# Transposes of the inverted blocks earlier in VectorE's order, and more streamed products ahead of the recursion and inside the attention levels of a GLA + RWKV-7 + expert layer

## The chip, the cores and the metric

The kernel runs on one core of one Trainium2 chip. The metric is the device time of one execution in microseconds; the median of several runs counts. TensorE (PE in the profile), VectorE (DVE), ScalarE (ACT), GpSimd (POOL) and SyncE (SP, which issues most of the DMAs) each work through their own queue in the order in which the program lists the instructions, and wait for one another through semaphores.

## What is computed

One layer on 256 tokens of width 2048. The input is multiplied by a wide matrix; one part of the columns feeds gated linear attention in two directions, one part feeds an RWKV-7 recursion in two directions, one part gives gates. Both results go through up-projections, an output projection and a layer norm; then 16 experts each choose 32 tokens (three matrices of 2048 x 1024 per expert), and a second layer norm ends it.

```
cols = x @ w_in                                   # 2048 x 10592
y_gla = gla(q, k, v, log_f) + rev(gla(rev(q), rev(k), rev(v), rev(log_b)))
y_rw  = rwkv7(r, w_f, k, v, -kk, kk*a) + rev(rwkv7(rev ...))
    # per token:  sa = S a_t;  S = S * w_t + sa b_t' + v_t k_t';  y_t = S r_t
merged = sigmoid(gate_gla) * (y_gla @ w_up_gla) + sigmoid(gate_rw) * (y_rw @ w_up_rwkv)
x = layer_norm(ALPHA * x + merged @ w_out)
x = layer_norm(ALPHA * x + expert_choice_ffn(x))  # 16 experts: w1, w3, w2
```

## The kernel before

**Two kinds of work.** The large projections (w_in, both up-projections, w_out) are *streamed products*: a generator, `stream`, walks a list of jobs. For each block of 128 rows of a weight matrix ScalarE rounds the block (`whi`, L238), VectorE subtracts to get the rest (`wlo`, L65 with output `wlo`), and TensorE makes three products from the two halves (L275 to L277 with 256 columns per product, or L284 to L286 with 512). The split of a block is put into the queues six blocks ahead of its products (`AHEAD`). The small, dependent work is the *chain*: four groups of four RWKV heads (`rwkv_group`, g = 0 to 3), then two pairs of GLA heads (`gla_pair`).

**How the order is set.** Nothing is scheduled by the compiler: the program order is written out. The chain is a generator that yields a number at each place where it would have to wait for another engine; `run_chain` hands that number to `pump`, which puts streamed products of about that many microseconds into the queues before the chain goes on. A yield may also step a second chain beside it (`side`: the preparation of the next group; `before`: the end of the last group). A larger yield therefore puts more streamed products between two steps of the chain, and these are then missing from what is left when both chains have ended: after them `need("gate7")` and the up-projections run with nothing in between.

**In a group.** Each group inverts triangular 64 x 64 blocks. VectorE solves the 16 x 16 diagonal blocks by substitution (L854 to L864). The result `xn` goes to DRAM (`sc2`) and comes back as 32 x 32 blocks in `nt`, both by DMAs from ScalarE's queue (L871, L876). In the meantime the loop of L867 yields 11 pieces of streamed products (`PIECES`, `SUBST / PIECES` = 1.31 us each); at i = 1 the store is issued, at i = 5 the load. After the loop two VectorE transposes (L881) fill the other half of `nt`, and TensorE combines the blocks: 64 products of 32 x 32 (L889), 64 more (L896), 32 (L910), 32 (L931), with copies by ScalarE and VectorE in between (L890, L897, L900, L912). The finished inverse is `ud`: VectorE's L922 and L937 and ScalarE's L924 and L939 write it. Then comes a yield (L940) and the recursion over four chunks, which begins with 8 products that read `ud` (L969).

```
        for i in range(PIECES):
            yield SUBST / PIECES + side(SIDE1 / PIECES)
```

**In a GLA pair.** Eight levels (L1155), each with two multiplications by VectorE (`scale`), two subtractions (`sums`), four exponentials by ScalarE (`exps`), four 128 x 128 products (L1169) and, from the second level on, two predicated copies by VectorE (L1175). There are two yields per level, 1.22 at L1163 ahead of the products and 0.87 at L1170 behind them.

**The last half.** When all jobs are done, the tokens are routed and the experts' weights are streamed through rings of buffers of 1 MB each; the first of them are loaded during the w_out products and right after (L135, L138, L139).

Of the kernel before, what the change touches and what calls it, by code (L numbers as in the profile page):

```python
# [54 lines left out]
def build(tc, x, w_in, gla_a_up_f, gla_a_bias_f, gla_a_up_b, gla_a_bias_b, gla_norm_g,  # L55
# [6 lines left out]
    mm, act, dve, pool = nc.tensor.matmul, nc.scalar.activation, nc.vector, nc.gpsimd  # L62
# [14 lines left out]
    def bank(tag):  # L77
        return psum.tile([128, 512], F32, tag=tag, name=tag, bufs=4)
# [7 lines left out]
    def S(shape, tag, bufs=1, dt=F32):  # L86
        return (mid if tag in ("t8", "t8b", "x16") else sp if tag in main_tags else cp).tile(shape, dt, tag=tag, name=tag, bufs=bufs)
# [111 lines left out]
    SPREAD, SIDE1, SIDE2, POST, SUBST, PIECES = 0.30, 12.00, 1.00, 1.35, 14.40, 11  # L199
# [558 lines left out]
    def rwkv_group(g, st, ahead, before):  # L758
# [17 lines left out]
        for d in range(2):  # L776
            for p in range(2):

                pvs = [bank("ax").rearrange("p (c f) -> p c f", c=4) for _ in range(2)]
                for c in range(4):  # L780
                    for h in range(2):
                        sl = slice(64 * h, 64 * h + 64)
# [8 lines left out]
            for b in range(2):  # L791
                sl = slice(32 * b, 32 * b + 32)
# [21 lines left out]
        for d in range(2):  # L814
            ps = bank("ax")
            pv = ps.rearrange("q (i p f) -> q i p f", i=4, p=2)
            for i in range(4):
                c = i if d == 0 else 3 - i
# [6 lines left out]
            for p in range(2):  # L825
                for c in range(4):
                    for h in range(2):
                        sl = slice(64 * h, 64 * h + 64)
# [16 lines left out]
        side = ahead()  # L845
# [18 lines left out]
            yield w + side(w * SPREAD)  # L864
        dve.memset(xn.rearrange("p r c -> p (r c)")[:, 16:768:49], 1.0)
        nt = S([128, 2, 16, 32], "t4", 3)
        for i in range(PIECES):  # L867
            yield SUBST / PIECES + side(SIDE1 / PIECES)
            if i == 1:
                for q in range(2):  # L870
                    nc.scalar.dma_start(sc2.rearrange("(q r c) -> q r c", r=32, c=32)[:, 16 * q:16 * q + 16, :],  # L871
                                        xn[64 * q:64 * q + 64, :, 16 - 16 * q:48 - 16 * q])
            if i == 5:

                for d in range(2):
                    nc.scalar.dma_start(nt[64 * d:64 * d + 64, d],  # L876
                                        sc2[32768 * d:32768 * d + 32768].rearrange("(m p c) -> p m c", p=64, c=32))
        flat = lambda t: t.rearrange("p m c -> p (m c)")
        for d in (1, 0):
            sl = slice(64 * d, 64 * d + 64)  # L880
            dve.transpose(flat(nt[sl, 1 - d]), flat(nt[sl, d]))  # L881
        quads = [(64 * d + 32 * b, slice(64 * d + 32 * b, 64 * d + 32 * b + 32)) for d in range(2) for b in range(2)]

        cu = S([128, 2, 16, 32], "t4", 3)
# [30 lines left out]
        for h in range(2):  # L915
            for b in range(2):
                sl = slice(32 * b, 32 * b + 32)
# [9 lines left out]
        for m in range(16):  # L927
            p, c, h = m // 8, m // 2 % 4, m % 2
# [3 lines left out]
        for d in range(2):  # L932
            t_ = slice(32 - 32 * d, 64 - 32 * d)
            for h in range(2):
# [2 lines left out]
                    dve.tensor_copy(ud[o, d, :, :, t_], pv[o])  # L937
                else:
                    act(ud[o, d, :, :, t_], pv[o], AF.Copy)  # L939
        yield 0.60  # L940

        sts = S([128, 2, 2, 128], "t2", T2B)
        yt = S([128, 4, 2, 64], "t2", T2B)
# [6 lines left out]
        for i in range(4):  # L950
            ch = [i, 3 - i]
            if i:
                pv = small()
                for p in range(2):
                    for d in range(2):
                        for h in range(2):
                            sl = slice(64 * h, 64 * h + 64)
# [7 lines left out]
            for p in range(2):  # L965
                for d in range(2):
                    for h in range(2):
                        sl = slice(64 * h, 64 * h + 64)
# [6 lines left out]
            if i < 3:  # L975
                pv = small()
                for d in range(2):
                    for p in range(2):
                        for h in range(2):
                            sl = slice(64 * h, 64 * h + 64)  # L980
# [10 lines left out]
            for d, p, h in dph:  # L991
                sl = slice(64 * h, 64 * h + 64)
                mm(y[sl, d, p, :], am[:, d, p, ch[d], h, 64:128], av[:, ch[d], p, h, :], start=(d + p == 0), stop=(i == 0),
                   skip_group_check=True)
            if i:
                for d, p, h in dph:
                    sl = slice(64 * h, 64 * h + 64)
# [68 lines left out]
    def gla_pair(hp, ld, ahead, side):  # L1066
# [36 lines left out]
        for h in range(2):  # L1103
            for j in range(2):
                sl = slice(j * 128, j * 128 + 128)
# [9 lines left out]
        def sums(s):  # L1115
            DFt, DBt = [S([128, 2, T], "t2p", 4) for _ in range(2)]
            if s == 128:
                tt(DFt[:, :, 0:128], Fc[:, :, 127:128].broadcast_to([128, 2, 128]), Fc[:, :, 0:128], OP.subtract)
                tt(DBt[:, :, 0:128], lg[1][1][:, :, 127:128].broadcast_to([128, 2, 128]), Bx[:, :, 0:128], OP.subtract)
            else:  # L1120
                n = 512 // (2 * s)
                tt(bl(DFt, s), bl(Fc, s), bl(Fc, s)[:, :, s - 1:s].broadcast_to([128, n, 2 * s]), OP.subtract)
                tt(bl(DBt, s), bl(Bx, s), bl(Bx, s)[:, :, s:s + 1].broadcast_to([128, n, 2 * s]), OP.subtract)
            return DFt, DBt

        def exps(s, DFt, DBt):
            qe, ke = [S([128, 2, T], "t2", T2B) for _ in range(2)]
            if s == 128:
                act(qe[:, :, 128:256], Fc[:, :, 128:256], AF.Exp, scale=IT)
                act(ke[:, :, 128:256], Bx[:, :, 128:256], AF.Exp, scale=IT)  # L1130
                act(qe[:, :, 0:128], DBt[:, :, 0:128], AF.Exp, scale=IT)
                act(ke[:, :, 0:128], DFt[:, :, 0:128], AF.Exp, scale=IT)
            else:
                act(bl(ke, s)[:, :, :s], bl(DFt, s)[:, :, :s], AF.Exp, scale=-IT)
                act(bl(ke, s)[:, :, s:], bl(DBt, s)[:, :, s:], AF.Exp, scale=IT)
                act(bl(qe, s)[:, :, s:], bl(DFt, s)[:, :, s:], AF.Exp, scale=IT)
                act(bl(qe, s)[:, :, :s], bl(DBt, s)[:, :, :s], AF.Exp, scale=-IT)
            return qe, ke

        def scale(qe, ke):  # L1140
            tt(ke, ke, k_, OP.mult)
            tt(qe, qe, q_, OP.mult)
            return qe, ke
# [11 lines left out]
        for li, s in enumerate(levels):  # L1155
            qe, ke = sc.pop(0)
            if li + 1 < len(levels):
                sc.append(scale(*ex.pop(0)))
            if li + 2 < len(levels):
                ex.append(exps(levels[li + 2], *df.pop(0)))  # L1160
            if li + 3 < len(levels):
                df.append(sums(levels[li + 3]))
            yield 1.22  # L1163
            ps = bank("ax")
            pv = ps.rearrange("p (h j f) -> p h j f", h=2, j=2)
            for h in range(2):
                for j in range(2):
                    iq = 1 - j if s == 128 else j
                    mm(pv[:, h, j, :], ke[:, h, j * 128:j * 128 + 128], qe[:, h, iq * 128:iq * 128 + 128], start=True, stop=True)  # L1169
            yield 0.87 + side(1.08)  # L1170
            for j in range(2):
                if s == 128:
                    act(att[:, :, j, (1 - j) * 128:(1 - j) * 128 + 128], pv[:, :, j, :], AF.Copy)
                else:
                    dve.copy_predicated(att[:, :, j, j * 128:j * 128 + 128],  # L1175
                                        gmask[:, li - 1:li, :].broadcast_to([128, 2, 128]), pv[:, :, j, :])
            if li == 4:
                nxt = ahead()
        yield side(1e9)
        pos = []  # L1180
        for h in range(2):
            po = bank("ax")
            for vh in range(2):
                for j in range(2):
                    c = h * 256 + vh * 128
# [69 lines left out]
    def all_chains():  # L1255
# [31 lines left out]
        for g in range(4):  # L1287
            yield from rwkv_group(g, state[g], ahead(g + 1), before)
            before = beside(rwkv_post(g, state[g]))
        yield from rwkv_post(3, state[3])  # L1290
        ld = yield from gla_pair(0, state[4]["ld"], lambda: gla_load(1), beside(load_y(1, "am", 1)))
        yield from gla_pair(1, ld, lambda: None, lambda us: 0.0)
        need("gate7")
        chain_pool.close()
# [60 lines left out]
    for r in range(CAP // 8):  # L1355
        sl = slice(r * 8, r * 8 + 8)
# [96 lines left out]
    for gq in range(4):  # L1453
# [38 lines left out]
        if gq == 3:  # L1492
# [7 lines left out]
            for dc in range(4):  # L1500
                sl = slice(dc * 512, dc * 512 + 512)
# [8 lines left out]
        for f, nf, c0, n in down_pieces(gq):  # L1510
            wt = [take() for _ in range(4)]
            for j in range(nf):
                fb = f + j
                for c in range(c0, c0 + n, 512):
                    m = min(512, n)
# [5 lines left out]
            for c in range(c0, c0 + n, 512):  # L1521
                m = min(512, n)
# [32 lines left out]
    for i in range(8):  # L1555
        t2, sl = i % 2, slice(i // 2 * 512, i // 2 * 512 + 512)
# [38 lines left out]
```

## Time and profile before

| | |
|---|---|
| median of 3 runs | 1849.82 us (1841.05 to 1851.86) |
| profiled execution, its own time | 1846.94 us |
| its span | 1845.2 us, so 1.7 us lie around it |
| TensorE busy | 1610.6 us (87%) |
| VectorE busy | 775.2 us (42%) |
| ScalarE busy | 549.7 us (30%) |
| mean granted clock of TensorE | 0.959 of full speed |
| HBM read | 543.24 MB |

The page describes one execution. Busy times are sums over the instructions of an engine; an idle time is put down to what ended it. A line of the timeline gives the start, the length, the engine and line, the operation with output and inputs, the count of merged instructions and, in brackets, the idle time before them with its releaser. A line "(+2 forms)" mixes shapes. L65 is a helper that records every `tensor_tensor`, so it has to be told apart by its tiles.

### The profile page before, as it was taken

Reading aid. Unit: us, or ns where it says so; the run is one execution under the profiler, and the core shown is the slowest. Engines: PE = TensorE matmul, PEld = TensorE weight load, DVE = VectorE, ACT = ScalarE, POOL = GpSimd, SP = SyncE. Lnnn points to the kernel's source line nnn. Section 1 sums busy time; section 2 is a strip of 40 time slices with the busy share of each in tenths; the row PEclk is TensorE's granted clock in tenths of the full one; section 3 lists DMA queues with packets and bytes.
Section 4 is the critical chain, followed back from the end, with each engine's and each line's share of the span. In section 5 each row is a group of like instructions: output and inputs, shape, how many; then the busy total and the mean of one; then the engine's idle time right before and its main releaser. Section 6 shows DMA issues by size and latency. Waiting matters only on the chain.

```text
span 1845.2 us, 27727 instructions
## 1 busy us (share of the span) xinstructions
PE 1610.6 (87%) x11255; PEld 960.0 (52%) x11255; DVE 775.2 (42%) x1400; ACT 549.7 (30%) x1081; POOL 16.4 (1%) x42
## 2 busy tenths in 40 slices
PE   8998999989999999999785998668996779966696
PEld 7997887778677778888631233112331113411122
DVE  6777676667659866665421303111012110111204
ACT  5566354455456755444310001000010000100001
POOL 0000000000000000000000000000000000000000
PEclk9999899999999999999899899889999899998998
DMA  7856363554556558787999999999999999999996
GB/s 210 247 152 191 87 192 111 154 138 139 153 146 209 177 188 272 283 305 253 367 405 422 421 420 420 421 420 421 421 420 421 421 420 421 421 421 420 410 411 248
DMA packets 203114, 561.84 MB, mean 304 GB/s; under 512 B 49804, under 2 KB 100422, under 8 KB 156522
## 3 DMA queue, kind: packets, MB, share of 16 engines
q1 hardware_dynamic: 185008, 557.70, 80.6%
q10 hardware_dynamic: 17978, 2.37, 0.8%
q8 instruction: 88, 1.44, 0.3%
q14 instruction: 40, 0.33, 0.0%
HBM read 543.24 MB, written 16.78 MB: 304 GB/s over the span
## 4 chain that ended last, share of the span: by engine, by line
DMA 43%; PE 19%; DVE 4%; ACT 1%; issue 1%; SPq 0%; DVEq 0%; ACTq 0%
DMA ring_a<-in_w_dram 19%; DMA ring<-in_w_dram 19%; DMA t8b<-in_w_dram 4%; PE mm L284 4%; PE mm L286 4%; PE mm L285 4%; PE mm L1517 2%; PE mm L1468 2%; DVE wlo L65 1%; PE ax L1387 1%; DVE t L65 1%; DVE t2p L65 0%; PE ax L1186 0%; DVE sig L1481 0%; ACT whi L238 0%
## 5 line engine op out<-in xcount | busy, mean ns | idle before, releaser
L65 DVE TENSOR_TENSOR wlo<-wraw,whi 128x512 fp32r<-128x512 f32 (+2 forms) x480 | 311.8, 666 | 194.7 <-ACT whi L238 192.8
L238 ACT ACTIVATE whi<-wraw 128x512 fp32r<-128x512 f32 (+2 forms) x480 | 282.6, 608 | 147.8 <-PE mm L286 63.8
L275 PE MATMUL mm<-x,whi 128*128 128x256 f32 x688 | 209.5, 305 | 3.3 <-ACT whi L238 3.3
L1468 PE MATMUL mm<-ring_a,x 128*32 128x512 f32 x776 | 154.7, 676 | 57.6 <-DMA ring_a<-in_w_dram 57.6
L277 PE MATMUL mm<-x,wlo 128*128 128x256 f32 x688 | 196.7, 286 | 1.5 <-issue 1.5
L276 PE MATMUL mm<-x,whi 128*128 128x256 f32 x688 | 196.8, 286 | 0.0
L1480 DVE TENSOR_SCALAR sig<-sig 64x512 f32<-64x512 f32 x16 | 6.8, 424 | 434.5 <-ACT sig L1478 434.5
L1517 PE MATMUL mm<-ring_a,hid 128*32 128x512 f32 (+1 forms) x524 | 163.6, 601 | 1.5 <-ACT sig L1478 1.3
L284 PE MATMUL mm<-whi,x 128*128 128x512 f32 x384 | 161.6, 421 | 0.0
L1468 PE MATMUL mm<-ring,x 128*32 128x512 f32 x592 | 117.7, 683 | 47.7 <-DMA ring<-in_w_dram 47.5
L285 PE MATMUL mm<-wlo,x 128*128 128x512 f32 x384 | 152.6, 397 | 0.0
L286 PE MATMUL mm<-whi,x 128*128 128x512 f32 x384 | 152.4, 397 | 0.0
L275 PEld LDWEIGHTS mm<-x,whi 128*128 128x128 f32 x688 | 132.9, 193 | 11.9 <-issue 4.1
L65 DVE TENSOR_TENSOR x<-x,ax 128x512 f32<-128x512 f32 (+1 forms) x34 | 22.2, 655 | 270.7 <-PE ax L1527 270.7
L276 PEld LDWEIGHTS mm<-x,whi 128*128 128x128 f32 x688 | 133.2, 194 | 3.2 <-issue 3.1
L277 PEld LDWEIGHTS mm<-x,wlo 128*128 128x128 f32 x688 | 133.2, 194 | 2.0 <-issue 1.7
L1478 ACT ACTIVATE sig<-mm 64x512 f32<-64x512 f32 x16 | 9.4, 588 | 406.5 <-PE mm L1468 406.5
L1517 PE MATMUL mm<-ring,hid 128*32 128x512 f32 x392 | 124.1, 594 | 1.5 <-DMA ring<-in_w_dram 0.8
L1468 PEld LDWEIGHTS mm<-ring_a,x 128*32 128x32 f32 x776 | 29.4, 116 | 162.6 <-DMA ring_a<-in_w_dram 109.3
L1517 PEld LDWEIGHTS mm<-ring_a,hid 128*32 128x32 f32 x524 | 46.2, 111 | 111.9 <-issue 94.7
L1524 ACT ACTIVATE eo<-mm 128x512 f32<-128x512 f32 (+1 forms) x17 | 9.7, 572 | 295.2 <-PE mm L1517 282.3
L1468 PEld LDWEIGHTS mm<-ring,x 128*32 128x32 f32 x592 | 23.5, 117 | 130.9 <-DMA ring<-in_w_dram 89.6
(348 smaller groups left out, 2142.3 us busy)
## 6 DMA issues: line engine op xcount, KB each, us to landing
ring_a<-in_w_dram SPq DMA_DIRECT2D x180, 1024.0 KB
ring<-in_w_dram SPq DMA_DIRECT2D x139, 1024.0 KB
wraw<-in_w_in_dram SPq DMA_DIRECT2D x112, 512.0 KB
t8b<-in_w_dram SPq DMA_DIRECT2D x39, 1024.0 KB
wraw<-in_w_in_dram SPq DMA_DIRECT2D x96, 256.0 KB
wraw<-in_w_out_dram SPq DMA_DIRECT2D x24, 512.0 KB
ring_a<-in_w_dram SPq DMA_DIRECT2D x22, 512.0 KB
wraw<-in_w_up_rwkv_dram SPq DMA_DIRECT2D x16, 512.0 KB
```

What stands on the lines that cost most here:

```text
L65: dve.tensor_tensor(out_, a, b, op=op)
L238: act(hi, raw, AF.Copy)
L275: mm(o, whi[:, sl], hi(k), start=(st0 and cb % 2 == 0), stop=False, skip_group_check=True)
L276: mm(o, whi[:, sl], lo(k), start=False, stop=False, skip_group_check=True)
L277: mm(o, wlo[:, sl], hi(k), start=False, stop=st1, skip_group_check=True)
L284: mm(o, hi(k)[:, sl], whi, start=st0, stop=False)
L285: mm(o, hi(k)[:, sl], wlo, start=False, stop=False)
L286: mm(o, lo(k)[:, sl], whi, start=False, stop=st1)
L1387: mm(ps[:, j * 128:j * 128 + 128], zn[t2][:, dq * 256 + j:dq * 256 + 256:2], ohf[:, t2, gq * 128:gq * 128 + 128], start=(t2 == 0), stop=(t ...
L1468: mm(ps[32 * q:32 * q + 32, :], xe[:, kb, e4 * 32:e4 * 32 + 32], wt[q // 2][:, k, (q % 2) * 512:(q % 2) * 512 + 512], start=(kb == 0), sto ...
L1517: mm(pss[c // 512][32 * e4:32 * e4 + 32, c % 512:c % 512 + m], hids[e4][:, fb % 4, fb // 4, :], wt[e4][:, j, c - c0:c - c0 + m], start=(fb ...
L1524: act(eo[:, 0:m], pss[c // 512][:, c % 512:c % 512 + m], AF.Copy)
```

## The change

Three edits. (1) The two transposes go into the loop of pieces: for the groups 0 to 2 they are recorded at i = 8, two pieces sooner than before; for group 3 the loop gets two more pieces and the transposes stand at i = 10, behind as many pieces as before. (2) The yield ahead of the recursion goes from 0.60 to 2.00. (3) The second yield of each GLA level goes from 0.87 to 1.60. From the first edit on the line numbers of the changed kernel are higher by one. No operation is added or taken out.

```
         nt = S([128, 2, 16, 32], "t4", 3)
-        for i in range(PIECES):
+        flat = lambda t: t.rearrange("p m c -> p (m c)")
+        for i in range(PIECES + 2 * (g == 3)):
             yield SUBST / PIECES + side(SIDE1 / PIECES)
...
-        flat = lambda t: t.rearrange("p m c -> p (m c)")
-        for d in (1, 0):
-            sl = slice(64 * d, 64 * d + 64)
-            dve.transpose(flat(nt[sl, 1 - d]), flat(nt[sl, d]))
+            if i == 8 + 2 * (g == 3):
+                for d in (1, 0):
+                    sl = slice(64 * d, 64 * d + 64)
+                    dve.transpose(flat(nt[sl, 1 - d]), flat(nt[sl, d]))
...
-        yield 0.60
+        yield 2.00
...
-            yield 0.87 + side(1.08)
+            yield 1.60 + side(1.08)
```

VectorE, group 0, around the transposes: rows with `-` are before, with `+` after. `wlo` is a split of the stream, `shs` and `shd` are the evacuation of a finished job, L731 belongs to the preparation of group 1.

```order
-L731 SCALAR_TENSOR_TENSOR t_2487<-ld,prm,t_2338 128x256 x2
-L65 TENSOR_TENSOR wlo<-wraw,whi 128x512 x2
-L65 TENSOR_TENSOR shs<-ppad 128x256
-L330 SCALAR_TENSOR_TENSOR shd<-shs,der,shd 128x256
-L881 STREAM_TRANSPOSE t_2269<-t_2269 64x512 x2
+L882 STREAM_TRANSPOSE t_2269<-t_2269 64x512 x2
+L731 SCALAR_TENSOR_TENSOR t_2489<-ld,prm,t_2338 128x256 x2
+L65 TENSOR_TENSOR wlo<-wraw,whi 128x512 x2
+L65 TENSOR_TENSOR shs<-ppad 128x256
+L330 SCALAR_TENSOR_TENSOR shd<-shs,der,shd 128x256
```

Six instructions that stood ahead of the transposes now stand behind them; in the groups 1 and 2 they are four (L731 twice and two splits). On TensorE the L889 products of group 0 keep their place.

TensorE, group 1, from the last products of the inversion (L931, L932 after the change) to the first of the recursion (L969, L970), before:

```order
L931 MATMUL ax_4230<-t4_3976,t2_4197 32x32 x32
L284 MATMUL mm_4150<-whi_3938,x16_89 128x512
L285 MATMUL mm_4150<-wlo_3939,x16_89 128x512
L286 MATMUL mm_4150<-whi_3938,x16_90 128x512
L969 MATMUL ax_4272<-t4_3390,ud_404 64x64 x8
```

The same place after:

```order
L932 MATMUL ax_4242<-t4_3992,t2_4212 32x32 x32
L284 MATMUL mm_4078<-whi_3956,x16_89 128x512
L285 MATMUL mm_4078<-wlo_3957,x16_89 128x512
L286 MATMUL mm_4078<-whi_3956,x16_90 128x512
L284 MATMUL mm_4077<-whi_3976,x16_89 128x512
L285 MATMUL mm_4077<-wlo_3977,x16_89 128x512
L286 MATMUL mm_4077<-whi_3976,x16_90 128x512
L284 MATMUL mm_4078<-whi_3976,x16_89 128x512
L285 MATMUL mm_4078<-wlo_3977,x16_89 128x512
L286 MATMUL mm_4078<-whi_3976,x16_90 128x512
L970 MATMUL ax_4294<-t4_3409,ud_404 64x64 x8
```

Three streamed products have become nine. Group 3 has the same counts; in the groups 0 and 2, whose streamed products are half as wide, six become eighteen.

VectorE, one level of the first GLA pair, from one set of predicated copies to the next, before:

```order
L1175 COPY_PREDICATED t_7336<-gmask,ax 128x2x128 x2
L65 TENSOR_TENSOR t_7506<-t_7506,ld 128x512
L65 TENSOR_TENSOR t_7505<-t_7505,ld 128x512
L65 TENSOR_TENSOR t2p<-av 128x512
L65 TENSOR_TENSOR t2p<-t_7334 128x512
L65 TENSOR_TENSOR wlo<-wraw,whi 128x512
L1175 COPY_PREDICATED t_7336<-gmask,ax 128x2x128 x2
```

The same level after:

```order
L1176 COPY_PREDICATED t_7418<-gmask,ax 128x2x128 x2
L65 TENSOR_TENSOR t_7591<-t_7591,ld 128x512
L65 TENSOR_TENSOR t_7590<-t_7590,ld 128x512
L65 TENSOR_TENSOR t2p<-av 128x512
L65 TENSOR_TENSOR t2p<-t_7416 128x512
L65 TENSOR_TENSOR wlo<-wraw,whi 128x512
L334 TENSOR_SCALAR shd<-shd 128x512
L65 TENSOR_TENSOR wlo<-wraw,whi 128x512
L1176 COPY_PREDICATED t_7418<-gmask,ax 128x2x128 x2
```

One more split stands in the level, and here also a step of a job's evacuation (L334) that came later before. On TensorE nine or twelve streamed products stood between the L1169 products of two levels; now there are twelve or fifteen. Behind the last chain TensorE's list held 459 streamed products of 512 columns up to the first transpose of the merged activations (L1237, L1238 after); now it holds 366.

## Rows read from the trace of the kernel before

**Rows 1.** The page, the span in 40 slices.

```profile
PE   8998999989999999999785998668996779966696
PEclk9999899999999999999899899889999899998998
DMA  7856363554556558787999999999999999999996
```

**Rows 2.** Stretches: us; busy PE, PEld, DVE, ACT, POOL; PEclk; DMA share; GB/s.

```profile
140.00:560.00 420.00, 395.10 (x4952) 334.04 (x4951) 285.55 (x558) 220.21 (x437) 2.75 (x10) 0.96 0.52 149
...
655.00:890.00 235.00, 234.10 (x1149) 196.46 (x1149) 142.29 (x242) 118.56 (x215) 0.00 (x0) 1.00 0.79 267
...
910.00:1800.00 890.00, 719.93 (x3389) 212.19 (x3390) 129.05 (x147) 51.05 (x102) 0.00 (x0) 0.95 1.01 419
```

**Rows 3.** Waits of PE from 100 to 900 us: us in total, times, longest.

```profile
PE ax L889 <- DVE t L881: 14.7, 4, 7.5
PE ax L1169 <- DVE t L65: 4.1, 7, 1.1
PE ax L969 <- DVE ud L937: 4.0, 8, 0.9
```

**Rows 4.** Timeline of PE at L889, groups 0 to 3.

```profile
181.63 1.92 PE L889 MATMUL ax<-t,moff 32*32 32x32 f32 x124 [7.51 <-DVE t L881]
...
284.98 1.20 PE L889 MATMUL ax<-t,moff 32*32 32x32 f32 x120 [1.69 <-DVE t L881]
...
388.71 1.02 PE L889 MATMUL ax<-t,moff 32*32 32x32 f32 x59 [4.24 <-DVE t L881]
...
482.19 0.25 PE L889 MATMUL ax<-t,moff 32*32 32x32 f32 x4 [0.76 <-DMA t<-sc]
483.74 1.50 PE L889 MATMUL ax<-t,moff 32*32 32x32 f32 x118 [1.30 <-DVE t L881]
```

**Rows 5.** Timeline of DVE: group 0, group 1 (one row), group 2.

```profile
176.05 0.87 DVE L731 SCALAR_TENSOR_TENSOR t<-ld,prm,t 128x256 f32<-128x256 f32 x2
...
180.87 1.44 DVE L881 STREAM_TRANSPOSE t<-t 64x512 f32<-64x512 f32 x2
...
280.21 0.88 DVE L731 SCALAR_TENSOR_TENSOR t<-ld,prm,t 128x256 f32<-128x256 f32 x2
...
383.95 0.88 DVE L731 SCALAR_TENSOR_TENSOR t<-ld,prm,t 128x256 f32<-128x256 f32 x2
...
387.95 1.44 DVE L881 STREAM_TRANSPOSE t<-t 64x512 f32<-64x512 f32 x2
```

**Rows 6.** DMA packets of ScalarE's queue (q10) from 383.2 to 383.5 us.

```profile
q10 hardware_dynamic: 20, 0.00, 5.3%
```

**Rows 7.** Stretches as in Rows 2, shorter.

```profile
167.00:174.00 7.00, 7.00 (x63) 6.87 (x61) 4.76 (x7) 5.59 (x11) 0.00 (x0) 1.00 0.63 164
181.60:187.30 5.70, 5.67 (x163) 5.38 (x167) 2.82 (x5) 2.66 (x5) 0.00 (x0) 0.50 0.01 4
197.60:204.40 6.80, 6.72 (x61) 5.93 (x61) 1.12 (x2) 2.43 (x6) 0.00 (x0) 0.50 0.07 23
286.30:289.70 3.40, 3.40 (x27) 3.18 (x31) 1.29 (x2) 2.24 (x4) 0.00 (x0) 0.51 0.28 104
402.00:405.00 3.00, 2.03 (x21) 1.58 (x22) 0.93 (x3) 1.22 (x4) 0.00 (x0) 1.00 0.63 175
680.00:710.00 30.00, 30.00 (x131) 24.19 (x130) 15.56 (x24) 18.46 (x31) 0.00 (x0) 1.00 0.71 223
```

**Rows 8.** Timeline of PE from L931 to L969, group 1.

```profile
298.64 0.75 PE L931 MATMUL ax<-t,t 32*32 32x32 f32 x64
...
301.17 0.32 PE L969 MATMUL ax<-t,ud 64*64 64x64 f32 x2 [0.87 <-DVE ud L937]
301.71 1.33 PE L969 MATMUL ax<-t,ud 64*64 64x64 f32 x14 [0.22 <-DVE ud L937]
```

**Rows 9.** The GLA pairs: one stretch as in Rows 2; timeline of DVE and PE in a level.

```profile
560.00:655.00 95.00, 88.92 (x440) 71.23 (x439) 86.03 (x158) 66.23 (x146) 0.00 (x0) 1.00 0.58 178
...
579.19 0.70 DVE L65 TENSOR_TENSOR wlo<-wraw,whi 128x512 fp32r<-128x512 f32 x1
...
578.23 1.13 PE L1169 MATMUL ax<-t,t 128*128 128x128 f32 x8 [1.06 <-DVE t L65]
```

## The prediction

> **What bounds the kernel now.** I read the slices of the page first, then the stretches, then TensorE's waits, and then the timelines at the places of the three edits. The slices show two halves [rows 1]: up to about 890 us TensorE is at eight or nine tenths nearly everywhere, behind that the DMA engines are full. The stretches put numbers to it [rows 2]. From 910 to 1800 us the DMA share is 1.01 at 419 GB/s: the experts' weights set the pace there, and the change touches nothing of that half. From 655 to 890 us, behind the chains, TensorE is busy 234.1 of 235 us while the DMA share is 0.79: there the streamed products set the pace. From 140 to 560 us, in the four groups, TensorE is busy 395.1 of 420 us, so 24.9 us are idle, and its mean granted clock is 0.96. [...]
>
> So the first half ends when TensorE has done a fixed amount of work, and ends sooner by every microsecond of its idle time or half speed that goes. The second half starts from the last streamed products and should move up as a whole. That is my step from a stall to the end: one to one.
>
> The waits [rows 3] name what the idle time belongs to: 14.7 us for the transposes (four waits), 4.0 us for `ud` ahead of the recursion, 4.1 us (seven waits) in the GLA levels.
>
> **The transposes, groups 0 to 2.** In group 0 VectorE came to L731 at 176.05 and to the transposes only at 180.87 [rows 5]; TensorE stood until 181.63 [rows 4]. With the six instructions behind them the transposes start at 176.05. TensorE needs the first alone, half of 1.44 us, so it goes on at 176.8: 4.8 us less. In group 1 the place is reached at 280.21 and both are done at 281.7, ahead of the 283.3 at which TensorE begins its wait of 1.69 us: 1.7 us less. In group 2 the place is reached at 383.95; the new order has one split more ahead of it, 0.70 us [rows 9], so the first is done at 385.4 where TensorE waited until 388.71: 3.3 us less.
>
> **Group 3.** The transposes stay behind as many pieces; two pieces of 1.31 us follow, so TensorE arrives 2.6 us later and the two waits of 0.76 (the block's landing) and 1.30 us are covered: 2.1 us less, with work that the tail then lacks. The first edit gives 4.8 + 1.7 + 3.3 + 2.1 = 11.9 us.
>
> **What comes late next.** In group 0 L731 (0.87 us), two splits (1.4 us) and a part of an evacuation, about 3 us together, now run between the transposes and VectorE's next chain step. In the profile they ran while TensorE stood. `ud` may then be late and some of the gain return as a wait at L969: between 0 and 3 us; VectorE has idle time there (busy 285.6 of 420 us in the stretch [rows 2]), so I take the middle, 1.5 us. In the groups 1 and 2 L731 and the splits are 2.3 us and I take nothing, as the four blocks from L889 to L931 leave VectorE longer than that.
>
> **Ahead of the recursion.** Six streamed products of 512 columns more per group, or twelve of 256. One of 512 takes 30/131 = 0.23 us, one of 256 columns 7.0/63 = 0.11 us [rows 7], so 1.4 us per group. TensorE's L969 waits for copies whose time does not depend on it: in group 1 from L931's end at 299.39 to L969's at 303.04 it has 3.65 us [rows 8], with three products in it. The idle time shown is 0.87 + 0.22 us; more hides in the 14 products that took 1.33 us. The gain per group lies between 1.0 (the 4.0 us over four groups) and 1.4: I take 1.25, 5.0 us in all.
>
> **The GLA levels.** Three products more per level on TensorE, 0.70 us, and half a split on VectorE, 0.35 us [rows 9]. VectorE is busy 86.0 of 95 us there and ends most of TensorE's waits [rows 3, 9], so a level in which TensorE waits becomes 0.35 us longer while TensorE does 0.70 us more: 0.35 us gained. With seven such waits that is 2.5 us, with those of other names up to the 6.1 us that TensorE idles in the whole stretch; if VectorE falls behind elsewhere, nothing. I take 3.0.
>
> **The clock.** In group 0 it was at half speed from 181.6 to 187.3, behind the stall of 7.51 us, and again from 197.6 to 204.4, behind the wait at L969; in group 1 from 286.3, behind the wait of 1.69 us [rows 7]. [...] The wait in group 2 at L969, as long as the others, brought no drop (402 to 405 us, 1.00) [rows 7]. So an idle spell of that kind does not decide alone, and I don't take it all back: 0.5 us in group 0 at L889, where 3 us of stall remain, two thirds of 5.1 us at the other L889 places, a third of 6.8 us at L969, as its small products stay: 0.5 + 3.4 + 2.3 = 6.2 us. Ends: 0 and 14.7.
>
> [...]
>
> **Queues that are moved past.** The added products bring their loads forward on SP's queue, in front of the GLA pairs' inputs; the DMA share of 0.52 in the groups and 0.58 in the GLA stretch [rows 2, 9] leaves room, and I cost it at nothing. If that cover went, a GLA pair would begin one load late.
>
> **The sum.** 11.9 - 1.5 + 5.0 + 3.0 + 6.2 = 24.6 us off the 1846.9 us of the profiled execution gives 1822.3. The median of the runs lies 2.9 us higher; I forecast 1823. With every term at its best end (11.9 + 5.6 + 6.1 + 14.7) it would be 1809.
>
> **Rivals.**
>
> *The waits move along (20%).* VectorE does no less, and its late work turns up at L896, L910 and L969. For it: in the GLA stretch it is the fuller engine. Against: outside it is busy two thirds of the time. Half of the first edit, 4 us of the second, no clock: 10 us less, 1837.
>
> *The end is set elsewhere (8%).* The fillers only leave the tail, and the tail is as long for another reason. For it: the second half is all DMA. Against: in the tail TensorE is busy without a gap, the DMA engines are not. 1847.
>
> *The transposes block VectorE (7%), slower.* Now a transpose can reach the head of the queue before its block has landed, and the splits behind it wait too. In group 2 packets of the load still ran between 383.2 and 383.5 [rows 6], half a microsecond ahead of 383.95. A landing 4 us later makes the place as bad as before; from there on each microsecond costs one, once TensorE has used up the six blocks split ahead. Landings 10 us later in three groups cost 3 x 6 = 18 us, less the 8 us of the other edits: 1857. Against: the load has kept to its time in all four groups. [...]
>
> **Chances and range.** My forecast holds with 65%, its own range 1811 to 1832. A measurement of this kernel tells about 1% from no change: faster by over 1% is below 1831.3. Nearly all of the forecast and a tenth of the first rival lie there: 0.65. Within 1%, where the rest of the first rival and the second lie: 0.28. Slower: 0.07. The range up to the first rival and a little beyond is 1811 to 1842.
>
> **What would show it.** Right: the four L889 waits on the transposes fall to under 1 us each; L969 waits under 0.5 us per group; from 140 to 560 us a mean clock of 0.98; the second half starts some 25 us sooner with the same DMA rate. Wrong: L889's idle time now ends on the DMA (third rival), comes back at L896 or L969 (first), or the DMA-bound half grows by what the first loses (second).

## The result and the profile after

The changed kernel takes 1819.51 us (median of 4 runs, 1815.26 to 1821.73); the kernel before, on the same chip, 1846.2 us (1841.05 to 1851.86). The ratio is 0.9854, with an interval from 0.9831 to 0.9876: 26.7 us less, where 1823 us and a sum of 24.6 us were forecast. The profiled execution took 1819.94 us with a span of 1818.2 us, 27.0 us less than the profiled one of before.

The page, the span in 40 slices, answers to [rows 1]; the eights of TensorE in the fourth and the ninth slice, where the groups 0 and 2 waited for their transposes, are nines now:

```profile
PE   8999999999999999999776997668986679966696
PEclk9999999999999999999899999889999899998998
```

The stretches (columns as in [rows 2]). Everything behind the groups comes sooner, so they are cut earlier:

```profile
140.00:545.00 405.00, 394.58 (x4996) 334.24 (x4995) 290.04 (x567) 225.65 (x449) 2.76 (x10) 0.99 0.56 159
...
635.00:866.00 231.00, 231.00 (x1158) 195.08 (x1158) 147.38 (x258) 118.54 (x221) 0.00 (x0) 1.00 0.79 265
886.00:1780.00 894.00, 725.48 (x3409) 212.75 (x3407) 127.98 (x146) 51.06 (x102) 0.00 (x0) 0.95 1.01 419
```

In the groups TensorE is now idle for 405.00 - 394.58 = 10.4 us instead of 24.9. The tail is still without a gap, and the half that the DMA engines pace runs at the same 419 GB/s. TensorE's waits from 100 to 890 us, against [rows 3]:

```profile
PE ax L1170 <- DVE t L65: 6.6, 2, 4.0
...
PE ax L890 <- DVE t L882: 5.4, 2, 2.9
...
PE ax L897 <- issue: 1.9, 2, 1.6
PE ax L783 <- DVE am L65: 1.9, 1, 1.9
```

The transposes' share fell from 14.7 to 5.4 us, the recursion's 4.0 us (now L970) left the list, and the GLA levels' 4.1 us in seven waits became 6.6 us in two, both ahead of the first level of a pair. The timeline of TensorE at L890, groups 0 to 3, against [rows 4]:

```profile
175.81 1.43 PE L890 MATMUL ax<-t,moff 32*32 32x32 f32 x106 [2.48 <-DVE t L882]
...
275.17 1.29 PE L890 MATMUL ax<-t,moff 32*32 32x32 f32 x128
...
372.03 1.29 PE L890 MATMUL ax<-t,moff 32*32 32x32 f32 x128
...
465.40 0.25 PE L890 MATMUL ax<-t,moff 32*32 32x32 f32 x4
...
468.58 1.25 PE L890 MATMUL ax<-t,moff 32*32 32x32 f32 x124 [2.93 <-DVE t L882]
```

Groups 1 and 2 wait no more, group 0 waits 2.48 us instead of 7.51. In group 3 the wait got longer. VectorE's transposes come there at 467.81, behind splits that wait for ScalarE (VectorE stands 3.60, 0.23 and 1.37 us ahead of them). ScalarE's timeline in that place:

```profile
453.65 1.34 ACTq L872 DMA_DIRECT2D sc<-xn  x2
...
460.48 1.32 ACTq L877 DMA_DIRECT2D t<-sc  x2
461.90 1.16 ACT L238 ACTIVATE whi<-wraw 128x512 fp32r<-128x512 f32 x2 [3.67 <-issue]
```

L877, the issue of the block's load, reads what the store writes: it comes at 460.48, 0.7 us behind the store's last packets (by 459.8). It stands in ScalarE's queue ahead of the roundings: ScalarE stood 3.67 us, 1.32 of them the issue itself (the rounding begins 0.1 us behind its end), and the splits of VectorE, the transposes and TensorE's products followed late. The kernel before has the same order, but there the load is issued 4.7 us behind the store and not 6.8:

```profile
471.96 1.34 ACTq L871 DMA_DIRECT2D sc<-xn  x2
...
476.66 1.32 ACTq L876 DMA_DIRECT2D t<-sc  x2
```

The DMA queues in the stretch in which the store's packets ran (packets, MB, share of the 16 engines), first after the change (456.5 to 460 us), then before it (473.5 to 476 us). q10 is ScalarE's queue with the store, q1 is SP's with the weights:

```profile
q1 hardware_dynamic: 477, 0.91, 67.5%
q10 hardware_dynamic: 2080, 0.26, 48.1%
```

```profile
q10 hardware_dynamic: 2057, 0.26, 69.4%
q1 hardware_dynamic: 82, 0.14, 14.9%
```

Before, the weights had 14.9% beside the store's 69.4%; after the change they had 67.5% beside its 48.1%, and the store took longer: its last packets ran 4.1 us behind its issue before (by 476.1 us) and 6.1 us after.

The first transpose of the merged activations comes 25.2 us sooner (770.13 to 744.92 us), and so do the first products of the routing (902.38 to 877.17). Counted on TensorE up to the routing, the tail behind the last pair's levels is 21.8 us shorter (244.78 to 222.94), the four groups are 16.9 us shorter (418.26 to 401.34), and the two GLA pairs are 14.3 us longer (120.87 to 135.21), since they now hold streamed products that the tail held; 0.8 us lie ahead of the groups. From the routing to the end it is 942.8 us before and 941.0 after.

### The profile page after: what moved, and what is told of

It is laid out like the page before. It is cut to its first block, busy times and chain, and to the rows that moved or that the text cites. A ratio compares the mean times of both kernels' runs of the same rounds, so it can differ in the third digit from the quotient of the medians.

```text
span 1818.2 us, 27708 instructions
## 1 busy us (share of the span) xinstructions
PE 1600.9 (88%) x11255; PEld 955.3 (53%) x11255; DVE 773.4 (43%) x1400; ACT 548.6 (30%) x1081; POOL 16.5 (1%) x42
## 4 chain that ended last, share of the span: by engine, by line
DMA 40%; PE 39%; DVE 5%; ACT 2%; issue 1%; SPq 0%; ACTq 0%; DVEq 0%
DMA ring<-in_w_dram 18%; DMA ring_a<-in_w_dram 17%; PE mm L284 7%; PE mm L285 6%; PE mm L286 6%; PE mm L1518 5%; DMA t8b<-in_w_dram 4%; PE mm L1469 2%; PE mm L275 2%; PE mm L277 1%; PE mm L276 1%; PE ax L1170 1%; DVE wlo L65 1%; DVE t L65 1%; ACT whi L238 1%
## 5 line engine op out<-in xcount | busy, mean ns | idle before, releaser
L275 PE MATMUL mm<-x,whi 128*128 128x256 f32 x688 | 206.9, 301 | 2.9 <-ACT whi L238 2.9
L277 PE MATMUL mm<-x,wlo 128*128 128x256 f32 x688 | 194.4, 283 | 0.8 <-issue 0.8
L276 PE MATMUL mm<-x,whi 128*128 128x256 f32 x688 | 194.7, 283 | 0.0
L275 PEld LDWEIGHTS mm<-x,whi 128*128 128x128 f32 x688 | 131.0, 190 | 12.3 <-issue 5.1
L276 PEld LDWEIGHTS mm<-x,whi 128*128 128x128 f32 x688 | 131.1, 191 | 2.9 <-issue 2.9
L277 PEld LDWEIGHTS mm<-x,wlo 128*128 128x128 f32 x688 | 131.0, 190 | 0.3 <-DVE wlo L65 0.3
```

The costliest lines, as they stand in the source:

```text
L275: mm(o, whi[:, sl], hi(k), start=(st0 and cb % 2 == 0), stop=False, skip_group_check=True)
L276: mm(o, whi[:, sl], lo(k), start=False, stop=False, skip_group_check=True)
L277: mm(o, wlo[:, sl], hi(k), start=False, stop=st1, skip_group_check=True)
```

## The experiments

Each kernel was timed beside the kernel before on its own chip; a ratio is to that.

**The three edits apart.** Each edit alone, and the first two together.

```
e1: only the loop with the transposes at i = 8 (i = 10 in group 3)
e2: only   -  yield 0.60              +  yield 2.00
e3: only   -  yield 0.87 + side(1.08) +  yield 1.60 + side(1.08)
e4: the change without the edit of e3
```

> The first edit alone. My reckoning (each edit stands by itself, TensorE's idle time goes one to one): 11.9 us of waits at L889, less 1.5 that come back at L969, plus about 4 us of clock: some 14 us less than before. Rival (the waits move along): the L969 and L896 waits grow by what L889 loses, 6 us less or none.

Measured: 1830.37 us, ratio 0.9929 (0.9909 to 0.9949), 13 us less than 1843.84.

> The second edit alone. My reckoning: 5 us of waits at L969 and about 2 us of clock, 7 us less than before. Rival (the products only leave the tail, and the chain gets longer by as much): no change.

Measured: 1835.79 us, ratio 0.9951 (0.9933 to 0.9968), 9 us less by the ratio, 8 by the medians. The waits of each, TensorE from 100 to 890 us; first e1, then e2:

```profile
PE ax L970 <- DVE ud L938: 3.5, 5, 1.7
...
PE ax L890 <- DVE t L882: 1.7, 1, 1.7
```

```profile
PE ax L889 <- DVE t L881: 16.2, 4, 6.9
```

Each edit removes its own wait and leaves the other's standing, with one exception, group 3. With the first edit alone TensorE comes to L890 there without a wait:

```profile
467.90 1.43 PE L890 MATMUL ax<-t,moff 32*32 32x32 f32 x128
```

With the second alone its waits there are 0.62 and 4.86 us instead of 0.76 and 1.30, and the load is issued 7.9 us behind the store; TensorE and ScalarE of e2:

```profile
476.78 1.45 PE L889 MATMUL ax<-t,moff 32*32 32x32 f32 x92 [4.86 <-DVE t L881]
```

```profile
460.74 1.34 ACTq L871 DMA_DIRECT2D sc<-xn  x2
468.68 1.32 ACTq L876 DMA_DIRECT2D t<-sc  x2
```

> The third edit alone. My reckoning: 3 us less than before. Rival, from the trace of the changed kernel (the first level of each GLA pair waits 2.6 and 4.0 us there, and the clock falls behind these waits): the levels lose what they gain, between no change and 3 us more than before; the first-level waits stand in this profile too.

Measured: 1845.06 us, ratio 1.0011 (0.9998 to 1.0024): nothing gained. TensorE in e3: its wait at the second pair's first level, and the stretch from that wait on.

```profile
636.21 2.05 PE L1169 MATMUL ax<-t,t 128*128 128x128 f32 x8 [3.75 <-DVE t L65]
```

```profile
635.40:642.20 6.80, 5.99 (x18) 5.15 (x19) 6.80 (x13) 5.58 (x16) 0.00 (x0) 0.50 0.41 114
```

Inside the levels TensorE's waits at L1169 fall from 4.1 to 1.1 us, but ahead of the second pair's first level it waits 3.75 us, where the kernel before waits 1.57, and in the stretch that begins in this wait it is at half speed for 6.8 us (granted clock 0.50, 5.99 us busy), which I estimate to cost half of the busy time, 3.0 us.

> The first and the second edit without the third. My reckoning: 21 us less than before, 3 us slower than the full change. Rival, as in the run with the third edit alone: the third edit is worth nothing or costs up to 3 us, so this one comes out equal to the full change or up to 3 us faster; if the first-level waits of the GLA pairs come from the third edit, they are gone here.

Measured: 1820.92 us, ratio 0.9871 (0.9856 to 0.9887), 22.9 us less by the medians. The first two add up within the intervals (13 + 9 = 22). The whole change has 0.9854 and, run again, 0.9857; the intervals overlap. So the third edit adds between nothing and about 3 us beside the others; in the profiles pairs and tail together are 360.4 us without it and 358.1 and 357.0 with it.

The first-level waits are not gone without the third edit. The first pair's in e1, then in e4:

```profile
549.78 1.49 PE L1170 MATMUL ax<-t,t 128*128 128x128 f32 x8 [2.22 <-DVE t L65]
```

```profile
545.63 2.04 PE L1170 MATMUL ax<-t,t 128*128 128x128 f32 x8 [2.62 <-DVE t L65]
```

Run by run, in us: TensorE's waits ahead of the first products of the inversion in group 3, the time from the store's issue to the load's there, and TensorE's wait ahead of the first level of each pair.

| run | edits in it | group 3 | store to load | pair 1 | pair 2 |
|---|---|---|---|---|---|
| before | none | 2.06 | 4.7 | 0.37 | 1.57 |
| e1 | first | none | 4.5 | 2.22 | 1.43 |
| e2 | second | 5.48 | 7.9 | 2.47 | 3.66 |
| e3 | third | 2.13 | 4.7 | 0.37 | 3.75 |
| e4 | first and second | 1.77 | 6.6 | 2.62 | 1.94 |
| the change | all | 2.93 | 6.8 | 2.61 | 4.01 |
| f1, the change again | all | 2.33 | 7.5 | 2.62 | 4.02 |

The late load of group 3 is in every run with the second edit and in no other (in the runs below it is 6.6 to 8.4 us). The wait ahead of the first pair comes with the first or the second edit, not with the third; the one ahead of the second pair grows with the second alone and with the third.

**The whole change again, and what is left in it.**

```
f1: the change
f2: ahead of the first level   -  yield 1.94               +  yield 5.00
f3: -  if i == 8 + 2 * (g == 3):   +  if i == 8:
f4: -  if i == 8 + 2 * (g == 3):   +  if i == 6 + 4 * (g == 3):
```

> The full change once more, on the chip of the next three kernels. Theory (the edits add up: 13 us for the transposes and 9 us for the recursion measured alone, nothing for the levels): 22 us less than before. Rival (the third edit is worth something only when the stalls ahead of it are gone): 25 to 27 us less.

Measured: 1820.14 us, 0.9857 (0.9834 to 0.9879).

> The full change, and the yield of 1.94 that stands one level ahead of the first products of a GLA pair is 5.00: about five halves more, 3.3 us of streamed products, in front of the first level of each pair. Theory (the first level waits for VectorE, 2.6 and 4.0 us in the changed kernel, because TensorE gets there too soon, and the clock falls behind both waits, 10.2 us at half speed): both waits fall under 1 us and most of the 5 us of clock come back, 8 us less than the full change. Rival (VectorE is the bound of the stage, and each added product brings a split that puts the first level off by as much): the waits stay above 2 us, no change.

Measured: 1816.81 us, 0.9844 (0.9819 to 0.9869), not to be told from f1. TensorE's waits in the pairs of f2:

```profile
PE ax L1170 <- DVE t L65: 2.9, 3, 1.0
PE ax L1187 <- DVE t L1176: 2.2, 1, 2.2
```

The two long waits at the first levels are gone, but 5.1 us stand at later levels and behind the last. Pairs and tail together are 357.1 us, as in f1 (357.0): filling this gap moved it. The waits fell as the theory had it, the time did not.

> The full change with the transposes of group 3 also at i = 8, four pieces ahead of the products that need them. Theory (the 2.9 us wait there comes from splits ahead of the transposes that wait for ScalarE): the wait falls to 1.5 us or less, and the drop of the clock behind it may go too, 1.5 to 3 us less than the full change. Rival (the blocks land too late for that): the wait is the same and ends on the DMA, no change.

Measured: 1818.51 us, 0.9849 (0.9824 to 0.9874). The wait of group 3 at L890 is gone from the list (L890 has one wait left, 2.5 us in group 0), the time is not to be told from f1. Most of the wait comes back a little further on, at L897 and L911 of the same group: 0.95 and 0.98 us, where f1 has 0.17. With the edit of f2 as well (g2):

> The full change with more products ahead of the first level (1.94 becomes 5.00) and with the transposes of group 3 at i = 8, both together. Theory (the GLA stage is bound by VectorE, so the first is worth at most the clock behind the first-level waits, 3 us; the second 2.9 us of wait): 3 to 5 us less than the full change. Rival (the waits move to other levels and to L897): no change.

Measured: 1816.65 us, 0.9846 (0.9826 to 0.9865): the lowest median of all, within the interval of the change itself. Here, too, there are waits at L897 and L911 of group 3 (1.46 and 0.98 us) and at later levels, as the rival has it.

> The full change with the transposes of the groups 0 to 2 at i = 6, one piece behind the issue of the load, so that they reach the head of VectorE's queue some 3 us ahead of the landing. Rival of the prediction (a transpose that waits for its blocks holds the splits and the chain behind it): VectorE idles 3 us per group on the DMA and TensorE loses about as much, 5 to 9 us slower than the full change. Theory (six blocks split ahead cover it): VectorE idles as long, TensorE does not, within 3 us of the full change.

Measured: 1826.25 us, 0.9887 (0.9859 to 0.9916), 6 us above f1; on the same chip each of its four runs (1821.70 to 1827.99) is slower than each of f1's (1816.61 to 1821.40). Group 1 of f4 shows the whole chain; the rows are of VectorE, of ScalarE, and of TensorE:

```profile
275.72 1.44 DVE L882 STREAM_TRANSPOSE t<-t 64x512 f32<-64x512 f32 x2 [3.07 <-DMA t<-sc]
277.10 1.19 DVE L716 TENSOR_TENSOR_SCAN t2p<-rstr,t2p 128x520 f32<-128x520 f32 x1
...
278.32 0.64 ACT L726 ACTIVATE t2p<-t2p 128x520 f32<-128x520 f32 x1 [3.18 <-DVE t2p L716]
...
283.08 0.57 ACT L891 ACTIVATE t<-ax 128x512 f32<-128x512 f32 x1
...
283.71 1.22 PE L897 MATMUL ax<-t,t 32*32 32x32 f32 x121 [1.40 <-ACT t L891]
```

VectorE stands 3.07 us on the load; the scan behind the transposes is late by that; ScalarE's L726 waits 3.18 us for the scan, and L891, which stands behind it in ScalarE's list, begins only at 283.08; TensorE, which has its L890 products done at 280.0, waits 1.40 us at L897. Over three groups VectorE loses 8.6 us to the load and TensorE 8.3 us at L897.

**Is VectorE the bound in the GLA pairs?** Two ways of taking 16 multiplications of 0.68 us off it; h1 leaves them out, so it computes something else:

```
g1: -  tt(ke, ke, k_, OP.mult)   +  pool.tensor_tensor(ke, ke, k_, op=OP.mult)
g3: g1 and f3 together
h1: -  tt(ke, ke, k_, OP.mult)   +  pass
```

> The full change, and one of the two multiplications of each GLA level (ke by k) on GpSimd instead of VectorE: VectorE loses 16 x 0.6 = 10 us of work in a stage in which it is busy without a gap between the first and the last level of a pair. Theory (VectorE is the bound of the GLA stage, so filler there only moves TensorE's idle time of about 6 us from one level to another): TensorE's waits in the levels and at the first levels fall from 6.6 to under 2 us, the drops of the clock behind the first-level waits go, 5 to 10 us less than the full change. Rival (the waits come from the length of a level's own chain of steps, not from VectorE's load; GpSimd takes 1.27 us for such an operation where VectorE takes 0.67): the waits stay or grow, no change or slower.

Measured: 1825.89 us, 0.9899 (0.9881 to 0.9917); the waits at L1170 grew to 11.0 us.

> The multiplication on GpSimd and the transposes of group 3 at i = 8. Theory: 7 to 12 us less than the full change, the fastest of all. Rival: as for the two parts, no change.

Measured: 1821.81 us, 0.9876 (0.9858 to 0.9894). Timelines of g1 in a level, GpSimd and then VectorE:

```profile
554.59 1.83 POOL L1142 TENSOR_TENSOR t<-t,ld 128x512 f32<-128x512 f32 x1 [2.28 <-DMA wraw<-in_w_in_dram]
559.97 1.82 POOL L1142 TENSOR_TENSOR t<-t,ld 128x512 f32<-128x512 f32 x1 [3.55 <-ACT t L1136]
```

```profile
554.59 2.38 DVE L65 TENSOR_TENSOR wlo<-wraw,whi 128x512 fp32r<-128x512 f32 x2
...
561.23 1.10 DVE L65 TENSOR_TENSOR t<-t,ld 128x512 f32<-128x512 f32 x1
```

Where GpSimd works, VectorE's two splits take 2.38 us instead of about 1.3, its multiplication 1.10 instead of 0.68; GpSimd's own takes 1.71 us in the mean over 16, against 1.27 for its two 128x512 instructions at L1565. So g1 gave VectorE's load back as longer instructions, and decides nothing about the bound. Hence h1:

> All three edits, and the multiplication of ke by k in the scaling of the GLA levels (one of the two there, 128x512, 0.68 us each on VectorE, 16 of them) is left out, so VectorE has 10.9 us less to do in the GLA pairs and GpSimd has nothing more. Theory (VectorE's work ends TensorE's waits in the GLA pairs after the third edit): TensorE's waits at L1170, 6.6 us with all three edits, fall under 2 us, the half-speed stretches behind the first levels (10.2 us) go, and the whole is 5 to 10 us shorter than with all three edits, about 1810 to 1815. Rival (the first level waits for the chain's own latency, whatever VectorE's load): the waits at L1170 stay at 5 us or more and the time stays at 1817 to 1821.

Measured: 1819.08 us, 0.9869 (0.9836 to 0.9902), the time of the whole change. TensorE's waits at L1170, two of 5.4 us together, and the eight levels of both pairs (columns as in [rows 2]):

```profile
545.21 1.47 PE L1170 MATMUL ax<-t,t 128*128 128x128 f32 x8 [2.01 <-DVE t L65]
...
617.89 2.05 PE L1170 MATMUL ax<-t,t 128*128 128x128 f32 x8 [3.41 <-DVE t L65]
```

```profile
545.20:574.80 29.60, 29.59 (x150) 25.07 (x151) 26.15 (x49) 20.63 (x46) 0.00 (x0) 0.94 0.75 235
617.90:647.30 29.40, 29.40 (x149) 25.07 (x150) 25.89 (x49) 20.69 (x46) 0.00 (x0) 0.95 0.59 179
```

The rival's numbers came. TensorE is busy 29.59 of 29.60 us in the levels, VectorE 26.15. With the third edit the levels are TensorE's, and taking work from VectorE buys nothing there. The two waits at the first levels stand ahead of them, in the preparation. There h1 takes out one multiplication per pair (the scaling of the first level stands ahead of the loop of levels), 0.68 us, and each wait is 0.60 us shorter (2.61 to 2.01, 4.01 to 3.41); in g1, where GpSimd does it in 1.8 us, they are 1.6 us longer than in f1 (4.18 and 5.65). So these two waits hang on VectorE's own instructions in the preparation, and not on latency alone, as the rival had it.

## Why the prediction was right, and where it was not

**One to one to the end: right.** The tail begins and ends without a gap, the first transpose of the merged activations comes 25.2 us sooner, the end 27.0 us. The 1.8 us between the two lie behind the routing, where nothing was changed: that part took 942.8 us before, 941.0 after, and 941.6 to 944.5 in the other profiles. So 25.2 us are the edits' and 1.8 are scatter. The rival by which the end is set elsewhere is out.

**The transposes: right in size, wrong in group 3.** Waits of 11.9 us and about 3.9 us of the clock, less 1.5, were to go, some 14; alone the edit gives 13. Group 0 keeps 2.48 us (3 was said), groups 1 and 2 none. The sign that I named, all four waits under 1 us, was stricter than my own sum, which left 3 us in group 0. That the two waits of group 3 "are covered" holds for the first edit alone (e1: no wait there), and fails beside the second: the wait went from 2.06 us (0.76 + 1.30) to 2.93. What failed is the term on the queues, "I cost it at nothing". With the second edit the load behind the store of group 3 is issued 6.6 to 8.4 us after the store instead of 4.5 to 4.7, and alone the edit makes the wait 5.48 us; in the profile of the change the weights had 67.5% of the DMA engines beside that store (14.9% before), ScalarE stood 3.67 us at L877, and the splits and the transposes came late on VectorE. That the late load comes from the second edit is shown by the runs; that it is the loads brought forward which slow the store is my reading of the two queues, and no run moves those loads by themselves. f3 removes the wait at L890, of which 1.9 us return at L897 and L911.

**The 1.5 us that I let return at L969: did not come** beside the second edit; no wait of L970 is left. Alone, the first edit leaves 3.5 us there (e1), no more than the 4.0 of before, though group 3's grew from 1.07 to 1.70. The rival by which waits move along is too large for the first two edits, which give 13 and 8 to 9 us by themselves, but its mechanism is there in all three: 2 us more ahead of the first GLA pair with either of the first two, group 3's wait with the second, and the second pair's first level with the third.

**Ahead of the recursion: right.** 5.0 us and 2.3 of the clock were forecast, 8 to 9 measured, with an interval from 6 to 12.

**The GLA levels: right inside them, wrong in front of them.** I wrote that "a level in which TensorE waits becomes 0.35 us longer while TensorE does 0.70 us more", and added that up over the levels to 3.0 us. The levels did close: alone the edit takes 3.0 us off their waits (e3), and in the whole change TensorE has no wait inside them any more. But the sum ended at the last level. Alone, the edit made the wait in front of the second pair's first level 2.2 us longer, the granted clock was 0.50 for 6.8 us from within that wait on, and the time is what it was. Beside the others it is worth nothing to 3 us. In the whole change the waits in front of the two first levels grew from 1.94 to 6.62 us, by 4.7, which I had at nothing; of these the first pair's 2.2 come with the first two edits (e1, e2, e4), not with the third. The timelines of TensorE in the profile of the whole change:

```profile
548.16 1.09 PE L1170 MATMUL ax<-t,t 128*128 128x128 f32 x4 [2.61 <-DVE t L65]
...
621.47 2.05 PE L1170 MATMUL ax<-t,t 128*128 128x128 f32 x8 [4.01 <-DVE t L65]
```

VectorE's instructions in the preparation set the length of these waits (h1 and g1), and its work inside the levels ahead does not: ahead of the second pair's wait h1 takes out the eight multiplications of the first pair and one in the preparation, and the wait falls by about one, 0.60 us. Why TensorE and VectorE come to this place some 2 us further apart in one run than in another is not settled; e2 waits 3.66 us ahead of the second pair and e4, which has the first edit as well, 1.94.

**The clock: right in size, by two errors.** 6.2 us were to come back. The stretches at half speed (a granted clock of 0.50) in the profile after, columns as in [rows 2]:

```profile
176.20:179.60 3.40, 3.40 (x110) 3.34 (x99) 3.04 (x7) 3.40 (x8) 0.00 (x0) 0.50 0.35 81
227.40:230.80 3.40, 3.40 (x47) 3.06 (x43) 2.25 (x5) 0.00 (x0) 0.00 (x0) 0.50 0.26 39
469.80:473.20 3.40, 3.40 (x10) 2.72 (x9) 1.66 (x4) 2.88 (x5) 0.00 (x0) 0.50 0.59 204
548.30:551.70 3.40, 3.40 (x13) 3.01 (x14) 3.40 (x7) 1.56 (x7) 0.00 (x0) 0.50 1.08 369
620.00:626.80 6.80, 5.33 (x17) 4.59 (x18) 6.80 (x13) 5.13 (x13) 0.00 (x0) 0.50 0.48 136
```

They last 20.4 us, 1.5 of it idle. The profile before has 34 us at a granted clock of 0.50 in the groups: those of [rows 7] and these, the first in the stall of group 0, the others behind L969 in group 1, L889 in the groups 2 and 3 and L969 in group 3:

```profile
177.00:181.60 4.60, 0.00 (x0) 0.00 (x0) 2.92 (x5) 2.58 (x6) 0.00 (x0) 0.51 0.55 171
...
303.40:306.80 3.40, 3.40 (x37) 2.54 (x36) 1.12 (x2) 1.64 (x5) 0.00 (x0) 0.50 0.16 18
...
388.70:392.10 3.40, 3.38 (x131) 3.32 (x132) 0.97 (x2) 1.42 (x3) 0.00 (x0) 0.51 0.21 78
...
484.30:487.70 3.40, 3.40 (x88) 2.73 (x74) 0.81 (x2) 2.21 (x4) 0.00 (x0) 0.50 0.49 175
...
501.40:504.80 3.40, 3.40 (x37) 2.76 (x36) 1.12 (x2) 1.84 (x5) 0.00 (x0) 0.50 0.00 0
```

What these stretches cost no run shows: the 14.7 us of the forecast, and the 5.1 at the L889 of the groups 1 to 3 and 6.8 at L969 of which it takes parts, are my estimate, half of the time at 0.50 outside the stall. The products come near it: those of 512 columns start 0.43 us apart at 0.50 (624.2 to 626.3 us in the profile after) and 0.23 us apart at 1.00 [rows 7]. By the same estimate the stretches after cost (20.4 - 1.5) / 2 = 9.5 us instead of 14.7: 5.2 us back. That this is near 6.2 is partly luck. In the groups 10.2 us are left, which cost 5.1: 9.6 us came back there. The other 10.2 us lie in the GLA pairs, where the clock was full before [rows 9], and cost 4.4 us that I had not counted. The first four follow a wait, 2.48 us in group 0, 1.85 at L783, 2.93 in group 3, 2.61 at the first pair's first level; the fifth begins in the 4.01 us at the second pair's. The wait at L783 (for VectorE's `am`), 1.85 us and 1.7 of the clock, I had not seen; before there are three there, 1.2 us in all and none over 0.6. The long one comes with the second edit (e2 and e4 have 1.86 us, e1 and e3 none over 0.6). A wait of 1.63 us at L897 in group 1 ("issue", cause open; the kernel before has such idle times elsewhere, 1.5 us at L277 and 0.9 at L910) brought no drop (granted clock 1.00 from 280 to 292 us). In the second run of the change (f1) the levels of the first pair ran at 1.00 (545.4 to 573.7 us) where the first has 0.94 (546.0 to 575.6), though the wait ahead of them is as long (2.62 and 2.61 us): this term moves by 3.4 us at half speed there from one execution to the next.

**The transposes block VectorE: the mechanism exists, the margin held.** f4 shows the rival at a place two pieces sooner: 8.6 us of VectorE's time on the load, 6 us of the whole. It did not show where I said. TensorE's idle time did not end on the DMA at L890 but on ScalarE at L897.

**The error in all:** 24.6 us against 25.2 up to the routing and 26.7 to 27.0 in all. The forecast of 1823 is not the sum that it is given with: 1822.3 us and the 2.9 by which the median lay higher make 1825.2. The sum is as near as that because its errors nearly cancel: the clock in the groups gave more than I said, and the waits ahead of the GLA pairs, the clock behind them and group 3, which I had at nothing or covered, took it back.

## What to carry to other kernels

VectorE and ScalarE went through their lists in order here, also where the next instruction had to wait (f4: VectorE stood 3.07 us at a transpose, and the scan behind it began at 277.10, as the transposes ended; ScalarE stood 3.18 us at L726, which reads the scan's result). So a dependent instruction had its best place just behind the time at which its input landed: in three groups TensorE waited 13.4 us for it with the transposes behind the loop and 2.5 us with them at i = 8, while at i = 6 the kernel lost 6 us, and this second cost came up two engines further on (i = 7 was not tried). When a wait is filled, follow the chain to the next place where it can be late, past the end of the loop: with the levels filled, the wait ahead of the next pair's first level grew, and behind that single wait (3.75 us in e3) the granted clock was 0.50 for 6.8 us. Edits that remove separate waits of the engine that sets the pace nearly add up here (13 and 9 us alone, 23 together), and could be sized from the waits' own rows; where they were not separate, in group 3, they met in a third place, by my reading the DMA engines. To see which edit makes a new wait, look for it in the run of each edit alone.

## What was not expected of the hardware

In g1 VectorE's instructions took longer where GpSimd's multiplication ran beside them. The split's mean went from 0.69 us (f1) to 0.84 us and the 128x512 multiplications from 0.68 to 0.88, so that of the 10.9 us of work taken off VectorE a good part came back: 53 splits took 43.2 us, where 56 took 36.8 in f1. VectorE's multiplication that began at 561.23 us ended at 562.33, where one of 0.68 us would have ended at 561.91, and the GpSimd instruction beside it (559.97, 1.82 us) ended at 561.79. Beside the GpSimd instruction at 554.59 the two splits ended at 556.97, 0.55 us behind its end at 556.42; at 561.23 it is 0.54 us. The longest split of g1 took 1.78 us in the pairs (0.70 in f1), and the mean of the six 128x512 instructions of L334 went from 0.42 to 0.68 us. What causes it no run shows.

A DMA issue whose data another DMA had yet to write held up ScalarE's arithmetic behind it: in the changed kernel ScalarE stood 3.67 us at L877 in group 3, and TensorE, behind VectorE's splits and transposes, 2.93 us.
